# A hybrid RWKV-7 / RG-LRU block: third and fourth lane start their products a step later, and the RG-LRU's last states are transposed elsewhere

## The chip, the core and the metric

One core of one Trainium2 chip runs the whole kernel. A core has a matrix engine (TensorE, PE in the rows), which multiplies out of the on-chip memory SBUF into eight banks of PSUM; VectorE (DVE), ScalarE (ACT) and GpSimd (POOL), which do elementwise work; and SyncE (SP), whose queue issues most of the DMAs between the chip's large memory and SBUF. Each engine has a queue of its own, in the order that the program gives it; an instruction that waits for another engine or for a DMA holds what stands behind it in its queue.

The metric is the device time of one execution in microseconds (us), taken as the median of several runs. Smaller is better.

## What is computed

One step of a diffusion backbone with one layer, on 128 context tokens and 1024 latent tokens (1152 in all, nine tiles of 128), model width 1024. Cut to what matters here:

```python
def block(x, cvec, s0, h0, grid, lp):
    mod = (jax.nn.silu(cvec) @ lp['w_mod'] + lp['b_mod'])[..., None, :]
    sh1, sc1, g1, sh2, sc2, g2 = jnp.split(mod, 6, axis=-1)
    h = rmsnorm(x, lp['ln1_g']) * (1.0 + sc1) + sh1
    proj = h @ lp['w_in']
    r, k, v, xw, xa, xg, xb, gb = jnp.split(proj, SPLITS, axis=-1)
    ya, s_fin = rwkv7_mix(r, k, v, xw, xa, xg, s0, lp['rw_w0'], lp['rw_w_up'], lp['rw_a0'], lp['rw_a_up'],
                          lp['rw_g_up'], lp['rw_k_k'], lp['rw_k_a'], lp['rw_r_k'], lp['rw_lnx_g'], lp['rw_lnx_b'])
    yb, h_fin = rglru_mix(xb, gb, h0, lp['lru_conv_w'], lp['lru_conv_b'], lp['lru_ga_w'], lp['lru_ga_b'],
                          lp['lru_gx_w'], lp['lru_gx_b'], lp['lru_lam'], grid)
    x = x + g1 * (jnp.concatenate([ya, yb], axis=-1) @ lp['w_out'])
    h = rmsnorm(x, lp['ln2_g']) * (1.0 + sc2) + sh2
    u = dwconv(h @ lp['w_up'], lp['ffn_conv_w'], lp['ffn_conv_b'], CONV_F_LEFT, grid)
    ua, ub = jnp.split(u, 2, axis=-1)
    x = x + g2 * ((jax.nn.gelu(ua) * ub) @ lp['w_down'])
    return x, s_fin, h_fin
```

`rwkv7_mix` is a scan over time for 8 heads of 64 in two directions, with one step

```python
def _wkv7_step(S, inp):
    r_t, w_t, kk_t, b_t, k_t, v_t = inp
    sa = jnp.einsum('dbhij,dbhj->dbhi', S, kk_t)
    S = S * w_t[..., None, :] - sa[..., :, None] * b_t[..., None, :] + v_t[..., :, None] * k_t[..., None, :]
    y = jnp.einsum('dbhij,dbhj->dbhi', S, r_t)
    return S, y
```

and `rglru_mix` is a convolution, gates and a linear scan, also in two directions. The block runs on the context from zero states and on the latents from cached states. The outputs are both normalised results, the context's final RWKV states (s_fin) and its final RG-LRU states (h_fin, new_state_lru, 1024 numbers).

## The kernel before

**Stages.** A first stage computes the input projection, and beside it the RG-LRU's scans and gates, the gate g of the RWKV half (products `lg`, copied into `gt`, spilled to `g_d`) and the first part of the RWKV recurrence. The second stage finishes the recurrence, and beside it computes the rest of the modulation (`md`, weights `wmod`), the norm and gate of finished RWKV tiles (`posts`) and the RG-LRU half of the output product (`wout_lru`, products `wo`, weights loaded as `wm` and split into a rounded `woh` and a rest `wol`). Then come the RWKV half of the output product (products `mm`, the mixed rows loaded as `yb`) with the second norm, and the feed-forward part.

**Lanes.** The eight heads are four pairs. A chain takes one pair through chunks of 128 tokens, in 64-row halves for two directions. Four lanes run such chains at once: a and b begin beside the projection, c and d with the second stage. For each step a lane loads `KR`, `TTp`, `VS` (`fetch`) and its keys `BK` (`fetch_keys`, which at its second call also copies KR into `kx` on ScalarE), and `prep` makes the step's own matrices: the product `p<-kx,BK` on TensorE, its mask `G` on VectorE, a scaling of BK on GpSimd, and in a second half the transposes of BK and their copy `Kt`. The chain proper then does products `y`, a solve `c<-R,TTp`, its copy back into `VS`, and the state's update `c<-VS,Kt`. The letter behind p, c, y, kx is the lane.

**Order.** Every part is written as a Python generator that gives way at each `yield`. `run_all` steps the generators of the second stage in proportion to the counts written beside them. The calls are recorded in that order, a scheduler then sets each engine's queue, and buffers and PSUM banks go round in the order in which they were asked for. In the second stage the `p` and `c` products of all four lanes share two banks (2 and 4):

```python
    deal(ya=(3,), yb=(5,), yc=(0,), yd=(1,), pa=two, pb=two, pc=two, pd=two, ca=two[::-1], cb=two[::-1], cc=two[::-1],
         cd=two[::-1], md=(6,), wo=(7,), po=two)
    run_all((lane_a, 98 - LA), (lane_b, 98 - LB), (lane_c, 26), (lane_d, 26), (posts(90), 90),
```

**The last states of the RG-LRU.** `lru_fin` (128 x 8) collects the context's last states. At the end of `rest_of_projection`, the last generator of the first stage, TensorE transposes it into a bank of `lg`, VectorE copies the 8 x 128 result to `lru_o`, and the sync engine spills it to the output.

Of the kernel before, what the change touches and what calls it, by code (L numbers as in the profile page):

```python
# [24 lines left out]
LA = 74  # L25
# [5 lines left out]
def beside_all(*gens):  # L31

    st = [[g, float(n), 0] for g, n in gens]
    while st:
        s = min(st, key=lambda e: e[2] / e[1])
        try:
            next(s[0])
            s[2] += 1
            yield
        except StopIteration:  # L40
            st.remove(s)


def run_all(*gens):
    for _ in beside_all(*gens):
        pass
# [12 lines left out]
def tile_hybrid_step(  # L59
# [9 lines left out]
    V, A, G, PE = nc.vector, nc.scalar, nc.gpsimd, nc.tensor  # L69
    load = nc.sync.dma_start  # L70
    spill = nc.sync.dma_start
# [13 lines left out]
    def bank(name):  # L85
        st = psum[name]
        i = st[0][st[1] % len(st[0])]
        st[1] += 1
        return ps_pool.tile([128, 512], F32, name=name, tag=f"b{i}", bufs=1)
# [28 lines left out]
    def half(i):  # L118
        return slice(64 * i, 64 * i + 64)

    def const(name, *shape):
        return cp.tile(list(shape), F32, name=name)
# [45 lines left out]
    def c2(name="c2", dt=F32):  # L168
        return pr.tile([128, 512], dt, name=name, tag="c2", bufs=NC2)
# [31 lines left out]
    ident = const("ident", 128, 128)  # L201
# [205 lines left out]
    for b in range(4):  # L407
        for j0 in (8, 0):
            ps = mod_mm(2 * b + (j0 == 0))
# [415 lines left out]
    lru_fin = const("lru_fin", 128, 8)  # L825
# [116 lines left out]
    class Background:  # L942


        def __init__(self):
            self.q, self.done = [], set()
# [44 lines left out]
    def rest_of_projection():  # L991
        gens = {"x": lru_x, "t": lru_gates, "g": lru_g, "p": p_xg}
        yield from beside([gens[e[0]](*[int(c) for c in e[1:]]) for e in SEQ], 0, RL, 0)
        while bg_l.step():
            yield
        ps = bank("lg")
        PE.transpose(ps[0:8, 0:128], lru_fin, ident)
        lo_ = c2("lru_o")[0:8, 0:128]
        V.tensor_copy(lo_, ps[0:8, 0:128])
        spill(new_lru.rearrange("a b d (q p) -> (a b d q) p", p=128), lo_)  # L1000


    rs = ExitStack()
# [23 lines left out]
    class Lane:  # L1027


        def __init__(self, pool, k, out=None):  # L1030
            self.out = out or pool
            self.pool, self.k, self.py, self.pc, self.pp = pool, k, "y" + k, "c" + k, "p" + k

        def ring(self, name, n, bufs=2):
# [23 lines left out]
    def fetch_keys(L, q, n_):  # L1058

        cs = slice(128 * n_, 128 * n_ + 128)  # L1060
        bk = L.ring("BK", 256).rearrange("p (d t) -> p d t", d=2)
        load(bk, kb_d[q.f, q.p, :, :, 1, cs])
        if n_ == 1:
            for e in range(2):
                A.activation(L.kx[half(e), :, :, e, :], q.KR[half(e)], AF.Copy)
        q.X[n_] = bk, L.kx[:, :, n_]
# [12 lines left out]
    def prep(L, q, n_):  # L1079

        gm = L.ring("G", 512).rearrange("p (d e t) -> p d e t", e=2, d=2)
        km = L.ring("Kt", 256)
        bk, kx = q.X.pop(n_)
        ps = bank(L.pp)
        for d in range(2):
            mm(ps[:, 256 * d:256 * d + 256], bk[:, d], kx[:, d].rearrange("p e t -> p (e t)"))
        V.tensor_tensor(gm, ps.rearrange("p (d e t) -> p d e t", e=2, d=2),
                        mask[:, :, n_].unsqueeze(2).to_broadcast([128, 2, 2, 128]), op=OP.mult)
        x = 2 * q.p + n_
        G.tensor_tensor(bk, bk, pc_f[q.f][:, :, x:x + 1].to_broadcast([128, 2, 128]), op=OP.mult)  # L1090
        yield
        ps = bank(L.pp)
        for d in range(2):
            PE.transpose(ps[:, 128 * d:128 * d + 128], bk[:, d], ident)
        A.activation(km, ps[:, 0:256], AF.Copy)
        q.G[n_] = gm
        q.K[n_] = km.rearrange("p (d t) -> p d t", d=2)
        yield

    def chain(L, pairs):  # L1100
# [8 lines left out]
        qs = {0: fetch(L, *pairs[0])}  # L1109
        fetch_keys(L, qs[0], 0)  # L1110
        fetch_keys(L, qs[0], 1)
        yield from prep(L, qs[0], 0)
        Sc = None
        for hi, (i, n_) in enumerate(hops):
            f, p = pairs[i]
# [7 lines left out]
            q = qs[i]  # L1123
# [11 lines left out]
            if n_ == 0 and (p < 2):  # L1135
                Sc = next_state()
                if p:
                    s_in = L.ring("Si", 128, 1).rearrange("p (d j) -> p d j", d=2)
                    load(s_in, ins["state_rwkv"][0, 0].rearrange("d (f e) i j -> f (e i) d j", e=2)[f])
                    ps = bank(L.pp)  # L1140
# [27 lines left out]
            ps = bank(L.pc)  # L1168
# [9 lines left out]
            if not last:  # L1178
                ps = bank(L.pc)
# [47 lines left out]
    E, LATE = range(1, 5), range(5, NT)  # L1227
    lane_a = chain(Lane(rp, "a"), [(0, p) for p in E] + [(f, 0) for f in range(4)] + [(2, p) for p in range(1, NT)])
    lane_b = chain(Lane(rp, "b"), [(1, p) for p in E] + [(3, p) for p in range(1, NT)])

    PB = 2
# [11 lines left out]
    LB = 52  # L1243
# [10 lines left out]
    pq = pqs.enter_context(tc.tile_pool(name="pq", bufs=1))  # L1254
# [3 lines left out]
    lcd = lcds.enter_context(tc.tile_pool(name="lcd", bufs=1, side="right"))  # L1258
# [3 lines left out]
    def of_output(name):  # L1262
        return pw if name in ("woh", "wol", "yb", "ybh", "ybl") else p3

    lane_c, lane_d = [chain(Lane(lcd, k, pq), [(f, p) for p in LATE]) for f, k in ((0, "c"), (1, "d"))]

    def p2(name, dt=F32, bufs=2):
        return of_output(name).tile([128, 512], dt, name=name, tag=name, bufs=bufs)
# [60 lines left out]
    def posts(n):  # L1329
        for _ in range(n):  # L1330
            bg_p.step()
            yield
# [55 lines left out]
    def mix_load(j, i):  # L1388
        y = p2("yb", bufs=YB)
        load(y.rearrange("p (f t) -> p f t", f=4),  # L1390
             y_d[4 * j:4 * j + 4, :, 128 * i:128 * i + 128].rearrange("f p t -> p f t"))
        return y
# [20 lines left out]
    def wout_lru():  # L1413

        wo = [wout_row(k, G) for k in range(4, 8)]
        yield
        y = mix_load(1, seq_t[0])
        for a, i in enumerate(seq_t):
            x = row4("x", XP)
            if a < 2:  # L1420
                g = gate_row(pw, 16, min(i, 1), "wo")
            load(x, x_rows(i))
            ys = mix_split(y)
            if a + 1 < NT:
                y = mix_load(1, seq_t[a + 1])
            yield
            for n_ in range(2):
                cs = slice(512 * n_, 512 * n_ + 512)
                ps = bank("wo")
                for k in range(4):  # L1430
                    mix_mm(ps, k, ys, wo, cs)
                    if k == 1:
                        yield
                gated(x[:, cs], p2("tm"), ps, g[:, cs])
                yield
            spill(xa_d[i], x)
        gate_last.append(g)
        for k in range(4):
            wo2.append(wout_row(k, G))
            yield  # L1440
# [1 line left out]
    two = (2, 4)  # L1442
    deal(ya=(3,), yb=(5,), yc=(0,), yd=(1,), pa=two, pb=two, pc=two, pd=two, ca=two[::-1], cb=two[::-1], cc=two[::-1],
         cd=two[::-1], md=(6,), wo=(7,), po=two)
    run_all((lane_a, 98 - LA), (lane_b, 98 - LB), (lane_c, 26), (lane_d, 26), (posts(90), 90),
            (seq(mod_rest(16, 24), beside_all((mod_rest(24, 48), 30), (wout_lru(), 48))), FL))
    bg_p.finish()
    p3x.close()
# [68 lines left out]
    for a, i in enumerate(seq_t):  # L1517
# [5 lines left out]
        for n_ in range(2):  # L1523
            ps = bank("mm")
# [184 lines left out]
    for m in range(NF):  # L1709
        q = Box()  # L1710
        q.m, q.ps = m, {}
        for j, c in first if m == 0 else usual:
# [9 lines left out]
            a, b = CH[c]  # L1722
# [10 lines left out]
    if True:  # L1733
# [17 lines left out]
        f = zf.rearrange("p i k t -> p (i k t)")  # L1751
        g2b, lnf, tm = f[:, 0:2 * D].rearrange("p (q c) -> p q c", q=2), f[:, 2 * D:3 * D], f[:, 3 * D:4 * D]
        load(lnf, ins["lnf_g"].unsqueeze(0).to_broadcast([128, D]))
        for q in range(2):
            for n_ in range(2):
                ps = bank("acc")
# [103 lines left out]
```

## Time and profile before

| what | value |
|---|---|
| median of three runs | 1854.52 us |
| the three runs | 1845.20, 1854.52, 1858.80 us |
| the profiled execution | 1849.17 us |
| its span, from the first to the last instruction | 1847.5 us |
| TensorE busy | 1716.4 us (93%) |
| VectorE, ScalarE, GpSimd busy | 69%, 47%, 39% |
| mean granted TensorE clock | 0.954 of full speed |
| DMA moved | 264.92 MB, 143 GB/s on average |

All rows come from the profiled execution. Its times count from the start of its span. The second stage lies from about 737 to about 957 us. A granted clock of 1.00 is the full clock of TensorE, 0.50 half of it; a figure between means that a stretch holds both.

### The profile page before, as it was taken

Reading aid. Unit: us, or ns where it says so; the run is one execution under the profiler, and the core shown is the slowest. Engines: PE = TensorE matmul, PEld = TensorE weight load, DVE = VectorE, ACT = ScalarE, POOL = GpSimd, SP = SyncE. Lnnn points to the kernel's source line nnn. Section 1 sums busy time; section 2 is a strip of 40 time slices with the busy share of each in tenths; the row PEclk is TensorE's granted clock in tenths of the full one; section 3 lists DMA queues with packets and bytes.
Section 4 is the critical chain, followed back from the end, with each engine's and each line's share of the span. In section 5 each row is a group of like instructions: output and inputs, shape, how many; then the busy total and the mean of one; then the engine's idle time right before and its main releaser. Section 6 shows DMA issues by size and latency. Waiting matters only on the chain.

```text
span 1847.5 us, 35759 instructions
## 1 busy us (share of the span) xinstructions
PE 1716.4 (93%) x13341; PEld 1442.9 (78%) x13341; DVE 1272.2 (69%) x2633; ACT 865.5 (47%) x1787; POOL 721.8 (39%) x742
## 2 busy tenths in 40 slices
PE   5998898888999989899988789999999998999996
PEld 4776676678777778456656689999999998888885
DVE  5458967797477664476788877676767667576764
ACT  6466655643666756333335844444444443121211
POOL 1022423322355344131121166666666663434340
PEclk8898979889999999899999899999999999999998
DMA  9254544443443434867775222222222225558571
GB/s 300 63 163 155 174 139 135 147 147 118 145 122 97 131 104 146 257 194 231 232 254 189 82 64 86 78 72 72 74 79 75 77 73 171 184 159 262 173 252 57
DMA packets 268428, 264.92 MB, mean 143 GB/s; under 512 B 21173, under 2 KB 218448, under 8 KB 268256
## 3 DMA queue, kind: packets, MB, share of 16 engines
q1 hardware_dynamic: 252496, 245.97, 42.1%
q10 hardware_dynamic: 15472, 16.54, 2.7%
q8 instruction: 105, 1.72, 0.4%
q14 instruction: 67, 0.55, 0.1%
q0 software_dynamic: 288, 0.14, 0.0%
HBM read 188.00 MB, written 74.58 MB: 142 GB/s over the span
## 4 chain that ended last, share of the span: by engine, by line
PE 66%; DVE 9%; ACT 3%; DMA 3%; issue 3%; POOL 3%; SPq 0%; ACTq 0%; POOLq 0%; DVEq 0%
PE acc L92 14%; PE x L92 7%; PE y L92 7%; PE z L92 7%; PE mm L92 7%; PE v L92 3%; PE wo L92 3%; PE ya L92 2%; PE lg L92 2%; PE md L92 2%; PE pa L92 2%; PE ca L92 1%; DVE X L501 1%; PE yb L92 1%; DVE gt L499 1%
## 5 line engine op out<-in xcount | busy, mean ns | idle before, releaser
L92 PE MATMUL mm<-h_hi,winp 128*128 128x384 f32 x1056 | 304.4, 358 | 4.9 <-DVE vr L808 3.2
L92 PEld LDWEIGHTS mm<-h_hi,winp 128*128 128x128 f32 x1056 | 198.7, 196 | 26.4 <-issue 14.9
L92 PE MATMUL mm<-h_lo,winp 128*128 128x384 f32 x528 | 187.7, 356 | 3.0 <-DVE h_lo L112 3.0
L112 POOL TENSOR_TENSOR wl<-raw,wh 128x512 fp32r<-128x512 f32 x110 | 155.1, 1412 | 69.7 <-ACT wh L106 69.4
L106 ACT ACTIVATE wh<-raw 128x512 fp32r<-128x512 f32 x110 | 69.5, 633 | 148.3 <-PE z L92 81.0
L92 PE MATMUL x<-f_hi,wh 128*128 128x256 f32 (+1 forms) x352 | 105.8, 301 | 8.9 <-ACT q L1652 5.3
L92 PEld LDWEIGHTS mm<-h_lo,winp 128*128 128x128 f32 x528 | 103.7, 197 | 9.6 <-DVE h_lo L112 4.5
L1090 POOL TENSOR_TENSOR BK<-BK,pc 128x256 f32<-128x256 f32 x72 | 47.8, 664 | 150.5 <-PE pa L92 58.8
L92 PE MATMUL x<-f_lo,wh 128*128 128x256 f32 (+1 forms) x352 | 105.5, 300 | 0.2 <-DVE f_lo L112 0.2
L92 PE MATMUL y<-t_hi,wh 128*128 128x320 f32 (+1 forms) x352 | 104.9, 298 | 0.7 <-DVE q L1657 0.7
L92 PE MATMUL x<-f_hi,wl 128*128 128x256 f32 (+1 forms) x352 | 105.3, 299 | 0.0
L92 PE MATMUL y<-t_lo,wh 128*128 128x320 f32 (+1 forms) x352 | 104.7, 297 | 0.0
L92 PE MATMUL y<-t_hi,wl 128*128 128x320 f32 (+1 forms) x352 | 104.6, 297 | 0.0
L112 POOL TENSOR_TENSOR wl<-S,wh 128x512 fp32r<-128x512 f32 x44 | 57.7, 1311 | 105.6 <-ACT wh L106 105.6
L92 PE MATMUL acc<-f_hi 128*128 128x512 f32 x330 | 91.0, 397 | 3.2 <-ACT zf L1760 3.2
L108 POOL TENSOR_SCALAR t_hi<-raw 128x512 fp32r<-128x512 f32 x66 | 52.9, 804 | 81.6 <-PE acc L92 35.4
L1619 DVE SCALAR_TENSOR_TENSOR zf<-C,fcw,zf 128x567 f32<-128x567 f32 x66 | 63.5, 962 | 23.3 <-ACT zf L1617 23.3
L92 PEld LDWEIGHTS acc<-f_hi 128*128 128x128 f32 x330 | 63.1, 192 | 16.9 <-ACT zf L1760 3.7
L92 PEld LDWEIGHTS x<-f_hi,wh 128*128 128x128 f32 x352 | 67.9, 193 | 9.9 <-ACT q L1652 5.8
L112 DVE TENSOR_TENSOR t_hi<-raw,t_hi 128x512 fp32r<-128x512 f32 x66 | 48.1, 735 | 37.0 <-POOL t_hi L108 37.0
L1617 ACT ACTIVATE zf<-C,colB,fcw 128x576 f32<-128x576 f32 x66 | 57.3, 868 | 28.1 <-DVE C L1689 15.7
L600 POOL TENSOR_TENSOR kd<-kd,rk 128x512 f32<-128x512 f32 (+1 forms) x24 | 32.2, 1342 | 97.0 <-ACT kd L598 96.8
(516 smaller groups left out, 5211.1 us busy)
## 6 DMA issues: line engine op xcount, KB each, us to landing
raw<-in_w_down SPq DMA_DIRECT2D x132, 256.0 KB, 3.1
raw<-in_w_up SPq DMA_DIRECT2D x88, 256.0 KB, 3.0
wmod<-in_w_mod SPq DMA_DIRECT2D x68, 256.0 KB, 4.2
act_d<-zf SPq DMA_DIRECT2D x44, 288.0 KB, 2.2
src<-act_d SPq DMA_DIRECT2D x66, 192.0 KB, 3.8
win<-in_w_in SPq DMA_DIRECT2D x44, 256.0 KB, 3.9
KR<-kb_d SPq DMA_DIRECT2D x36, 256.0 KB, 3.2
VS<-v_d SPq DMA_DIRECT2D x36, 256.0 KB, 3.2
```

What stands on the lines that cost most here:

```text
L92: PE.matmul(out, lhsT, rhs, start=start, stop=stop, skip_group_check=True)
L106: A.activation(hi, src, AF.Copy)
L108: eng.tensor_scalar(hi, src, 1.0, 0.0, op0=OP.mult, op1=OP.add)
L112: eng.tensor_tensor(lo, src, hi.bitcast(F32), op=OP.subtract)
L499: V.tensor_tensor(tv, X[:, q + 1:32, q:q + 1].to_broadcast([128, m, q]), X[:, q:q + 1, 0:q].to_broadcast([128, m, q]), op=OP.mult)
L501: V.tensor_tensor(X[:, q + 1:32, 0:q], X[:, q + 1:32, 0:q], tv, op=OP.add)
L600: G.tensor_tensor(self.kd, self.kd, self.k, op=OP.mult)
L1090: G.tensor_tensor(bk, bk, pc_f[q.f][:, :, x:x + 1].to_broadcast([128, 2, 128]), op=OP.mult)
L1617: A.activation(u, src, AF.Identity, scale=fcw[:, 1, m:m + 1], bias=colb("ffn_conv_b", m))
L1619: V.scalar_tensor_tensor(dv[:, :, 1:64], sv[:, :, 0:63], fcw[:, 0, m:m + 1], dv[:, :, 1:64], op0=OP.mult, op1=OP.add)
```

## The change

Two edits. The transpose, copy and spill of `lru_fin` leave the end of the first stage and come, behind a step of their own, between the output weights and the first load of mixed rows in `wout_lru`; they use the `wo` bank and a buffer of `tm`. And a lane can be given a lag: lanes c and d, with a lag of 1, issue their first loads, give way once, and only then record their first `prep`. Their step counts in `run_all` go from 26 to 27.

```diff
--- before.py
+++ after.py
@@ -993,11 +993,6 @@
         yield from beside([gens[e[0]](*[int(c) for c in e[1:]]) for e in SEQ], 0, RL, 0)
         while bg_l.step():
             yield
-        ps = bank("lg")
-        PE.transpose(ps[0:8, 0:128], lru_fin, ident)
-        lo_ = c2("lru_o")[0:8, 0:128]
-        V.tensor_copy(lo_, ps[0:8, 0:128])
-        spill(new_lru.rearrange("a b d (q p) -> (a b d q) p", p=128), lo_)
 
 
     rs = ExitStack()
@@ -1027,8 +1022,10 @@
     class Lane:
 
 
-        def __init__(self, pool, k, out=None):
+        def __init__(self, pool, k, out=None, lag=0):
             self.out = out or pool
+
+            self.lag = lag
             self.pool, self.k, self.py, self.pc, self.pp = pool, k, "y" + k, "c" + k, "p" + k
 
         def ring(self, name, n, bufs=2):
@@ -1109,6 +1106,8 @@
         qs = {0: fetch(L, *pairs[0])}
         fetch_keys(L, qs[0], 0)
         fetch_keys(L, qs[0], 1)
+        for _ in range(L.lag):
+            yield
         yield from prep(L, qs[0], 0)
         Sc = None
         for hi, (i, n_) in enumerate(hops):
@@ -1262,7 +1261,7 @@
     def of_output(name):
         return pw if name in ("woh", "wol", "yb", "ybh", "ybl") else p3
 
-    lane_c, lane_d = [chain(Lane(lcd, k, pq), [(f, p) for p in LATE]) for f, k in ((0, "c"), (1, "d"))]
+    lane_c, lane_d = [chain(Lane(lcd, k, pq, 1), [(f, p) for p in LATE]) for f, k in ((0, "c"), (1, "d"))]
 
     def p2(name, dt=F32, bufs=2):
         return of_output(name).tile([128, 512], dt, name=name, tag=name, bufs=bufs)
@@ -1414,6 +1413,12 @@
 
         wo = [wout_row(k, G) for k in range(4, 8)]
         yield
+        ps = bank("wo")
+        PE.transpose(ps[0:8, 0:128], lru_fin, ident)
+        fin = p2("tm")[0:8, 0:128]
+        V.tensor_copy(fin, ps[0:8, 0:128])
+        spill(new_lru.rearrange("a b d (q p) -> (a b d q) p", p=128), fin)
+        yield
         y = mix_load(1, seq_t[0])
         for a, i in enumerate(seq_t):
             x = row4("x", XP)
@@ -1442,7 +1447,7 @@
     two = (2, 4)
     deal(ya=(3,), yb=(5,), yc=(0,), yd=(1,), pa=two, pb=two, pc=two, pd=two, ca=two[::-1], cb=two[::-1], cc=two[::-1],
          cd=two[::-1], md=(6,), wo=(7,), po=two)
-    run_all((lane_a, 98 - LA), (lane_b, 98 - LB), (lane_c, 26), (lane_d, 26), (posts(90), 90),
+    run_all((lane_a, 98 - LA), (lane_b, 98 - LB), (lane_c, 27), (lane_d, 27), (posts(90), 90),
             (seq(mod_rest(16, 24), beside_all((mod_rest(24, 48), 30), (wout_lru(), 48))), FL))
     bg_p.finish()
     p3x.close()
```

No instruction is added or removed. What the edits do to the queues is seen in the order of the built programs (no time is in it; each row gives line, operation, output<-inputs, size, count).

TensorE before, at the join of the two stages. The `lg` products and the transpose of `lru_fin` are the last rows of the first stage; pc and pd are first products and transposes of lanes c and d:

```order
L92 MATMUL lg<-sgh,guph 128x384
L92 MATMUL lg<-sgl,guph 128x384
L92 MATMUL lg<-sgh,gupl 128x384
L997 MATMUL lg<-ident,lru_fin 8x128
L92 MATMUL pc<-kxc,BK 128x256 x2
L1094 MATMUL pc<-ident,BK 128x128 x2
L92 MATMUL pd<-kxd,BK 128x256 x2
L1094 MATMUL pd<-ident,BK 128x128 x2
L92 MATMUL pa<-kxa,BK 128x256
L92 MATMUL ca<-R,TTp 64x64 x2
L92 MATMUL md<-wmod,silx 32x512 x2
L92 MATMUL ca<-R,TTp 64x64 x2
```

TensorE after, at the end of the `lg` products:

```order
L1091 MATMUL pb<-ident,BK 128x128 x2
L92 MATMUL ca<-R,TTp 64x64 x2
L92 MATMUL lg<-sgh,guph 128x384
L92 MATMUL lg<-sgl,guph 128x384
L92 MATMUL lg<-sgh,gupl 128x384
L92 MATMUL yb<-S1b,KR 128x128 x2
L92 MATMUL yb<-VS,G 64x64 x4
L92 MATMUL ca<-R,TTp 64x64 x2
L1417 MATMUL wo<-ident,lru_fin 8x128
L92 MATMUL ya<-VS,G 64x64
L92 MATMUL pb<-kxb,BK 128x256 x2
```

and, eight rows on, at the join:

```order
L92 MATMUL lg<-sgh,guph 128x384
L92 MATMUL lg<-sgl,guph 128x384
L92 MATMUL lg<-sgh,gupl 128x384
L92 MATMUL ya<-VS,G 64x64
L92 MATMUL pc<-kxc,BK 128x256 x2
L92 MATMUL pd<-kxd,BK 128x256 x2
L92 MATMUL md<-wmod,silx 32x512 x3
L92 MATMUL pa<-kxa,BK 128x256 x2
L92 MATMUL md<-wmod,silx 32x512
L92 MATMUL cb<-R,TTp 64x64 x4
```

Steps of lanes a and b (ca, ya, pb) and the transpose moved ahead of the last `lg` products; pc and pd follow each other, and their transposes stand further back, among md products.

The sync engine's queue before, from the last spills of `g_d` to lane d's first loads. The first two BK are lane c's, the KR, TTp, VS and BK behind them lane d's:

```order
L773 DMA g_d<-gt 128x1152 x2
L940 DMA y_d<-th 128x1152
L773 DMA g_d<-gt 128x1152 x2
L1000 DMA out<-lru_o 8x128
L1272 DMA lnx<-in_rw_lnx_g 128x512
L1272 DMA lnx<-in_rw_lnx_b 128x512
L1062 DMA BK<-kb_d 128x2x128 x2
L1051 DMA KR<-kb_d 128x2x256
L1052 DMA TTp<-tt_d 128x256
L1054 DMA VS<-v_d 128x2x256
L1062 DMA BK<-kb_d 128x2x128 x2
```

The same queue after. The BK ahead of the second pair of `g_d` spills is lane c's first:

```order
L773 DMA g_d<-gt 128x1152 x2
L940 DMA y_d<-th 128x1152
L1059 DMA BK<-kb_d 128x2x128
L773 DMA g_d<-gt 128x1152 x2
L1271 DMA lnx<-in_rw_lnx_g 128x512
L1271 DMA lnx<-in_rw_lnx_b 128x512
L1059 DMA BK<-kb_d 128x2x128
L1048 DMA KR<-kb_d 128x2x256
L1049 DMA TTp<-tt_d 128x256
L1051 DMA VS<-v_d 128x2x256
L1059 DMA BK<-kb_d 128x2x128 x2
```

One load of keys moved ahead of two spills, and the spill of `lru_o` went away.

The sync engine's queue before, at the last output weights (`wm`) of the second stage and the first mixed rows (`yb`) of the next:

```order
L1381 DMA wm<-in_w_out 128x512
L1324 DMA y_d<-gd 128x2x128
L1381 DMA wm<-in_w_out 128x512 x2
L1436 DMA xa_d<-x 128x1024
L1286 DMA gd<-g_d 128x2x128
L1381 DMA wm<-in_w_out 128x512 x2
L1324 DMA y_d<-gd 128x2x128
L1390 DMA yb<-y_d 128x4x128
L1511 DMA x<-xa_d 128x1024
```

and after:

```order
L1389 DMA yb<-y_d 128x4x128 x2
L1441 DMA xa_d<-x 128x1024
L1340 DMA wmod<-in_w_mod 128x512 x2
L1285 DMA gd<-g_d 128x2x128
L1284 DMA v<-v_d 128x2x128
L1323 DMA y_d<-gd 128x2x128
L1516 DMA x<-xa_d 128x1024
L1380 DMA wm<-in_w_out 128x512
L1285 DMA gd<-g_d 128x2x128
L1380 DMA wm<-in_w_out 128x512
L1441 DMA xa_d<-x 128x1024
L1380 DMA wm<-in_w_out 128x512 x3
```

The first two yb stand ahead of the last five wm, and the last spill xa_d is followed by three wm where it was followed by two.

## Rows read from the trace of the kernel before

**Rows 1.** The profile's page, part 1: busy time, share of the span, instructions.

```profile
PE 1716.4 (93%) x13341; PEld 1442.9 (78%) x13341; DVE 1272.2 (69%) x2633; ACT 865.5 (47%) x1787; POOL 721.8 (39%) x742
```

**Rows 2.** Windows: length, TensorE busy (instructions), granted clock, DMA share, GB/s.

```profile
736.00:744.00 8.00, 1.24 (x6) 0.71 0.91 296
744.00:755.00 11.00, 9.49 (x32) 0.59 0.74 239
755.00:776.00 21.00, 21.00 (x147) 1.00 0.75 237
776.00:806.00 30.00, 25.55 (x250) 0.94 0.57 184
806.00:957.00 151.00, 150.70 (x1250) 1.00 0.74 237
957.00:985.00 28.00, 16.73 (x69) 0.76 0.77 246
```

**Rows 3.** Timeline of TensorE: start, duration, line, output<-inputs, shapes, count [idle before, releaser].

```profile
733.86 0.45 PE L92 MATMUL lg<-sgh,guph 128*128 128x384 f32 x1 [1.64 <-ACT gt L771]
...
736.61 0.27 PE L997 MATMUL lg<-ident,lru_fin 128*8 128x128 f32 x1
743.63 2.05 PE L92 MATMUL pc<-kxc,BK 128*128 128x256 f32 x4 [6.76 <-DMA BK<-kb_d]
746.44 0.69 PE L1094 MATMUL pc<-ident,BK 128*128 128x128 f32 x2 [0.75 <-DVE G L1087]
...
749.58 0.69 PE L1094 MATMUL pd<-ident,BK 128*128 128x128 f32 x2 [0.75 <-DMA wmod<-in_w_mod]
...
751.05 0.48 PE L92 MATMUL ca<-R,TTp 64*64 64x64 f32 x4
...
755.31 1.13 PE L92 MATMUL pb<-kxb,BK 128*128 128x256 f32 x4
...
768.27 1.13 PE L92 MATMUL pc<-kxc,BK 128*128 128x256 f32 x4
```

**Rows 4.** Timeline of the sync engine's queue, 732 to 743 us.

```profile
732.44 0.32 SPq L940 DMA_DIRECT2D y_d<-th  x1
...
737.57 0.30 SPq L1000 DMA_DIRECT2D out<-lru_o  x1
...
738.97 1.19 SPq L1062 DMA_DIRECT2D BK<-kb_d  x2
740.20 0.61 SPq L1051 DMA_DIRECT2D KR<-kb_d  x1
...
741.98 1.18 SPq L1062 DMA_DIRECT2D BK<-kb_d  x2
```

**Rows 5.** DMA issues, 725 to 750 us: count, KB each, median us to landing.

```profile
BK<-kb_d SPq DMA_DIRECT2D x5, 128.0 KB, 4.5
```

**Rows 6.** Timeline of ScalarE, 732 to 754 us.

```profile
732.27 0.56 ACT L1075 ACTIVATE R<-yb 64x128 f32<-64x128 f32 x2 [1.17 <-PE yb L92]
...
744.75 1.28 ACT L1065 ACTIVATE kxd<-KR 64x512 f32<-64x512 f32 x2 [3.62 <-DMA KR<-kb_d]
...
753.56 0.57 ACT L1075 ACTIVATE VS<-ca 64x128 f32<-64x128 f32 x2 [2.87 <-PE ca L92]
```

**Rows 7.** Timeline of GpSimd, around the first rounding of output weights.

```profile
792.82 0.62 POOL L1090 TENSOR_TENSOR BK<-BK,pc 128x256 f32<-128x256 f32 x1 [4.68 <-PE pb L92]
793.40 2.22 POOL L108 TENSOR_SCALAR woh<-wm 128x512 fp32r<-128x512 f32 x3
```

**Rows 8.** Timeline of TensorE, first products of the next stage.

```profile
967.61 0.76 PE L92 MATMUL mm<-woh,ybh 128*128 128x512 f32 x1 [4.83 <-ACT rv L128]
...
970.05 0.79 PE L92 MATMUL mm<-woh,ybl 128*128 128x512 f32 x1 [1.25 <-DVE ybl L112]
```

**Rows 9.** Timeline of the sync engine's queue, last output weights.

```profile
956.57 0.91 SPq L1381 DMA_DIRECT2D wm<-in_w_out  x2
958.63 0.33 SPq L1436 DMA_DIRECT2D xa_d<-x  x1
```

## The prediction

> **What bounds the kernel now.** I read the page's engine table first: TensorE is busy for 93% of the span and no other engine for more than 69% [rows 1]. So time can only be won where TensorE waits or runs at the lower clock, and only if nothing later takes the gain back. The windows show where that is [rows 2]. From 806 to 957 us, most of the stage of the four lanes, TensorE is busy for 150.70 of 151 us at full clock, and from 755 to 776 all the time. Three stretches that the diff touches are not dense: the join of the projection and this stage (736 to 755 us: busy 1.24 of 8 and 9.49 of 11 us, clocks 0.71 and 0.59), the start of the RG-LRU's output product (776 to 806 us: 25.55 of 30) and the hand-over to the next stage (957 to 985 us: 16.73 of 28).
>
> TensorE's timeline names the waits of the join [rows 3]. Work ends with the transpose of lru_fin at 736.88. The next instruction, lane c's first product, starts at 743.63 after 6.76 us of idling that ended when its keys BK had landed. Lane c's transposes wait 0.75 us for G, then lane d's product and transposes follow with another 0.75, and only behind them come steps of lanes a and b (ca, pb), although lane b's R had been copied at 732.27 [rows 6]. They stand there since the four lanes share two banks, in program order. Behind the idle time the clock is lower: pc's four instructions take 2.05 us, against 1.13 at 768.27.
>
> The sync engine's queue says why BK was late [rows 4]. It is issued at 738.97, behind the spills of g, the spill of lru_o and two loads of norm rows; pc starts 4.66 us later, and the transfers of this stretch list 4.5 us to landing for BK's 128 KB [rows 5], with the DMA engines 91% busy from 736 to 744 [rows 2].
>
> **The change part by part.** *RG-LRU's last states.* The same transpose (0.27 us), the same small copy and the same 4 KB spill are issued elsewhere. On the sync engine the spill leaves the place ahead of lane c's and d's loads: 0.30 us of issue, 0.47 to the start of the next row [rows 4]. On TensorE the transpose falls into the wait of 1.64 us before 733.86 [rows 3]. In its new place the spill stands on the sync engine between loads of the output weights and waits there for its copy on VectorE; wmod loads, output-weight loads, yb and a load of keys are queued behind it. GpSimd begins to round the first of these weights at 793.40 only [rows 7], and the transpose that feeds the copy stands among the lg products, so I cost the wait at nothing. Without that cover it costs the lateness of one copy of 8 rows, below 1 us.
>
> *Lanes c and d a step later.* In the changed order lane a's ca and ya and lane b's pb stand among the last lg products, pc and pd directly behind each other, and their transposes some fifteen rows later among md products. On the sync engine's queue lane c's first keys stand ahead of the last two spills of g. The sum by steps:
>
> 1. End of lg. Lane a's ca (0.48 for half of it, so 0.96 at most), pb (1.13) and the transpose (0.27) come among the lg products: 2.36 us, of which 0.27 stood at their end before and 1.64 fills the wait for gt [rows 3]. So lg ends some 0.5 us later, at about 737.4. ScalarE's copies of VS (0.57, rows 6 show them at 753.56) come ahead of the last gt and can put these off by as much.
> 2. pc. BK is issued behind y_d, at 732.44 + 0.32 = 732.8, and lands 4.66 later, at 737.4. So pc follows lg with hardly a gap, at full clock (1.13), and ends at 738.5.
> 3. pd. It stands next and nothing passes it. It needs lane d's KR, the copy kxd, and its keys. KR was issued at 740.20, the copy began 4.55 later, when it had landed, and took 1.28 [rows 4, 6]. Ahead of KR the queue loses the lru_o spill (0.47) and one BK (half of 1.19) and gets up to 0.57 from step 1: issue at about 739.7, copy done at 745.5. Lane d's keys go out 1.78 us behind KR as before, at 741.5, and land at 746.0 by 4.5. I take 745.7. So the gap isn't closed. It moves from pc to pd and is as long (738.5 to 745.7, 7.2 us against 6.76), and I expect the lower clock behind it again.
> 4. Sum. Work starts again 745.7 − 743.63 = 2.1 us later, but less stands behind the gap: pc (2.05), two waits for transposes (0.75 each, now beside md products), ca (0.96) and pb (1.13), 5.6 us. The join gives **−3.5 us**. Its ends: 0, if lane d's last operand lands 3.5 us later than I take, as the last of a full DMA; and −9, if it arrives with lane c's (6.76 + 1.5 + 0.9 of clock on pc).
>
> Behind 755 TensorE is dense, so what is saved there stays saved unless a new wait appears.
>
> *The start of the output product.* The first rounding at 793.40 stands on GpSimd behind a BK of lane b that waited 4.68 us for pb [rows 7]; the changed order has this BK behind the first rounding. TensorE idles for 30 − 25.55 = 4.45 us in the stretch [rows 2], the most that can come back, and a new order can add as much. I take −0.5.
>
> *The hand-over.* The first product of the next stage waits 4.83 us, the first that reads ybl 1.25 [rows 8]. In the changed order the first two yb are issued ahead of the last five weight loads, which could win up to 6.1; against that the last spill xa_d stands ahead of three weight loads, where it was two. I take −0.5, between −6.1 and +4 (rival C).
>
> In all −4.5 us. The profiled execution took 1849.17 us, 1.67 more than its span and 5.35 less than the median of 1854.52 (runs from 1845.20 to 1858.80). That makes 1844.7 for such an execution and **1850** for the median.
>
> A rule bears on the gap. After 6.76 us without work the granted clock was 0.59, after the wait of 1.64 us no instruction shows a lower one [rows 2, 3]. The Trainium skill, page "TensorE: Matmul & The Clock Gate", section "Why this matters for your kernels", says to keep matmuls back to back, as waits for a DMA between them bring the clock down; the trace agrees. By it nothing of the clock is won here, since the gap stays as long, while a clock that stayed up would make the sum about 2 us better (0.9 for each of two lanes' products).
>
> **The rivals.** *(A) The gap moves and nothing is won.* For it: the DMA engines are 91% busy from 736 to 744, so lane d's last operand may come with the same last byte whatever the order, and products put ahead can delay gt and with it the g spills ahead of KR. Against: ca and pb have their data early and run in a gap that exists. That the new order only renames who waits belongs here. Result 0: 1854.5.
>
> *(B) The later waits go too.* An earlier first rounding lets output products fill 776 to 806, and early yb closes the hand-over's waits: −3.5 − 0.7 × 4.45 − 0.7 × 6.1, about −11: 1843.5. For it GpSimd's rows. Against: TensorE had work for 25.55 of these 30 us, so a lane's chain through other engines and not the weights may set the waits.
>
> *(C) Slower, by the hand-over.* The last weights come through three buffers. With xa_d ahead of three loads, the sixth waits for the last tile's sum: from about 957.0 (the second of the pair at 956.57) to behind xa_d, 958.63 + 0.33 [rows 9], 2 us, and the two behind it lose 2 us more to their round trips, while the join gives nothing: +4, 1858.5. It decides from the point where the last weights, and no longer yb, are what the first products of the next stage wait for.
>
> **How the numbers follow.** My forecast has 0.50, (A) 0.22, (B) 0.13, (C) 0.15. The likeliest gives 1850; its steps are uncertain by about 3 us, and a median of three runs by some 4, as the spread of the runs shows. The range that holds 8 in 10 reaches from a little beyond (B) to a little beyond (C): 1841 to 1860. One per cent of 1854.5, about what a measurement of this kernel can tell from no change, is 18.5 us. No case gets there: the waits of the three stretches, with 2 us of clock, are 6.8 + 1.5 + 1.6 + 2 + 4.5 + 6.1, some 22 us, and nearly all would have to go. Faster by over 1% gets 0.05, slower 0.03, for waits that no row of before shows and for uneven runs; 0.92 is within.
>
> **What would show it.** Right: pc starts before 738.5 and takes 1.1 us; a gap of 6 to 8 us stands before pd and is ended by kxd or BK; a clock near 0.6 follows it; pb's product of 755.31 stands before 737; the dense stretch that ended near 957 ends 3 to 4 us sooner. Wrong: if pd starts before 743, the gain is twice mine; if lg ends after 739 or pd starts after 748, there is none; if the first rounding of output weights stays near 793, (B) is out; if the first product of the next stage waits for wol or woh, (C) is in.

## The result and the profile after

The changed kernel takes 1863.12 us in the median of 12 runs (1855.86 to 1867.12), the kernel before 1852.98 us (1845.2 to 1858.8). The ratio is 1.0051, with a 95% interval of 1.0034 to 1.0067: 10 us slower, outside the range that I gave and against its sign. The profiled execution took 1860.33 us, its span is 1858.6.

The page's engine line after, and TensorE's windows (length, busy and instructions, clock, DMA share, GB/s) for the join, the dense stretch behind it, the start of the output product, the rest of the stage, and the hand-over:

```profile
PE 1719.8 (93%) x13341; PEld 1442.7 (78%) x13341; DVE 1273.7 (69%) x2633; ACT 864.1 (46%) x1787; POOL 719.2 (39%) x742
```

```profile
741.00:758.00 17.00, 8.72 (x33) 0.70 0.85 286
758.00:784.00 26.00, 26.00 (x168) 1.00 0.89 277
784.00:810.00 26.00, 20.05 (x148) 0.80 0.31 100
810.00:958.00 148.00, 147.98 (x1249) 1.00 0.75 238
958.00:1001.00 43.00, 27.86 (x163) 0.84 0.63 202
```

Read against [rows 2], with one shift: the last product of the projection, in a part with the same instructions in both kernels, starts at 729.8 here and at 723.6 before. So 6.2 us of the two profiles' distance of 11.1 arise before the change begins. The stretch of 806 to 957 us was dense before and is dense now. The stretch of small products behind the join is worse than before: 5.95 us idle in 26 at a clock of 0.80, where it was 4.45 in 30 at 0.94.

TensorE's timeline at the join and at the hand-over, the counterpart of [rows 3, 8] (6.2 us are to be taken off for the join):

```profile
738.59 0.27 PE L1417 MATMUL wo<-ident,lru_fin 128*8 128x128 f32 x1
...
743.66 1.13 PE L92 MATMUL pc<-kxc,BK 128*128 128x256 f32 x4
...
752.66 2.05 PE L92 MATMUL pd<-kxd,BK 128*128 128x256 f32 x4 [7.87 <-DMA BK<-kb_d]
...
969.61 0.48 PE L92 MATMUL mm<-woh,ybh 128*128 128x512 f32 x1
...
981.22 0.80 PE L92 MATMUL mm<-woh,ybl 128*128 128x512 f32 x1 [10.47 <-DVE ybl L112]
```

Pc no longer waits, pd does; and the first products of the next stage start at once, but the third of them waits 10.47 us for ybl, in the place of 4.83 and 1.25 before. (Mixed rows yb are split like the weights, into a rounded ybh and a rest ybl, which VectorE makes.) The sync engine's queue and ScalarE at the join ([rows 4, 6]):

```profile
738.95 0.52 SPq L1059 DMA_DIRECT2D BK<-kb_d  x1
...
741.98 2.37 SPq L773 DMA_DIRECT2D g_d<-gt  x2
...
746.41 0.61 SPq L1048 DMA_DIRECT2D KR<-kb_d  x1
...
748.19 1.18 SPq L1059 DMA_DIRECT2D BK<-kb_d  x2
```

```profile
750.93 1.28 ACT L1062 ACTIVATE kxd<-KR 64x512 f32<-64x512 f32 x2 [1.12 <-DMA KR<-kb_d]
```

The last states in their new place, their copy on VectorE and the spill in the sync engine's queue:

```profile
780.89 0.27 DVE L1419 COPY tm<-wo 8x128 f32<-8x128 f32 x1
```

```profile
782.34 0.47 SPq L1285 DMA_DIRECT2D gd<-g_d  x1
782.90 0.30 SPq L1420 DMA_DIRECT2D out<-tm  x1
```

The copy was done at 781.16, 1.7 us before the queue came to the spill, so the spill held nothing up.

GpSimd at the start of the output product ([rows 7]), and VectorE's last weight and ybl at the hand-over:

```profile
785.27 0.62 POOL L108 TENSOR_SCALAR woh<-wm 128x512 fp32r<-128x512 f32 x1
800.04 0.63 POOL L1087 TENSOR_TENSOR BK<-BK,pc 128x256 f32<-128x256 f32 x1 [14.15 <-PE pb L92]
800.64 1.20 POOL L108 TENSOR_SCALAR woh<-wm 128x512 fp32r<-128x512 f32 x2
```

```profile
978.54 0.68 DVE L112 TENSOR_TENSOR wol<-wm,woh 128x512 fp32r<-128x512 f32 x1
...
980.49 0.68 DVE L112 TENSOR_TENSOR ybl<-yb,ybh 128x512 fp32r<-128x512 f32 x1
```

One weight half is rounded 14 us earlier than before (by the shift), and the next stands behind a BK that waits 14.15 us for pb, so nothing is won by it. At the hand-over ybl stands in VectorE's queue behind the last rest of the weights, wol.

### The profile page after: what moved, and what is told of

It is laid out like the page before. It is cut to its first block, busy times and chain, and to the rows that moved or that the text cites. A ratio compares the mean times of both kernels' runs of the same rounds, so it can differ in the third digit from the quotient of the medians.

```text
span 1858.6 us, 35758 instructions
## 1 busy us (share of the span) xinstructions
PE 1719.8 (93%) x13341; PEld 1442.7 (78%) x13341; DVE 1273.7 (69%) x2633; ACT 864.1 (46%) x1787; POOL 719.2 (39%) x742
## 4 chain that ended last, share of the span: by engine, by line
PE 67%; DVE 8%; ACT 4%; POOL 2%; DMA 2%; issue 2%; SPq 0%; ACTq 0%; POOLq 0%; DVEq 0%
PE acc L92 14%; PE mm L92 7%; PE x L92 7%; PE y L92 7%; PE z L92 7%; PE v L92 3%; PE wo L92 3%; PE md L92 2%; PE lg L92 2%; PE ya L92 2%; PE pa L92 2%; PE yb L92 2%; PE ca L92 1%; PE pb L92 1%; DVE gt L499 1%
```

## The experiments

All ratios are to the kernel before, measured beside each on the same chip, with their 95% intervals. "Idle" is TensorE's idle time from one microsecond before the end of the last output product wo to the 48th product mm of the next stage, and "runs" is into how many unbroken runs the 64 md products of the stage fall in TensorE's queue. The kernels e1, e3, e6, e7, e9, e11, e13, e15 and the change have the lag.

| kernel | ratio | idle at the hand-over, us | runs |
|---|---|---|---|
| the change | 1.0051 [1.0034, 1.0067] | 15.1 | 33 |
| the change, again (e12) | 1.0057 [1.0037, 1.0077] | 16.4 | 33 |
| lag alone (e1) | 1.0016 [0.9999, 1.0032] | 11.8 | 31 |
| last states moved, with their step, alone (e2) | 1.0034 [1.0015, 1.0052] | 15.7 | 34 |
| both, without the added step (e3) | 1.0033 [1.0017, 1.0049] | 11.1 | 33 |
| before with a bare step (e5) | 1.0056 [1.0036, 1.0076] | 14.4 | 37 |
| change, first yb ahead of the spill (e6) | 1.0042 [1.0025, 1.0060] | 14.8 | 32 |
| change, spill on ScalarE's queue (e7) | 1.0020 [1.0006, 1.0034] | 16.0 | 32 |
| before, first loads of c and d from ScalarE (e8) | 1.0024 [1.0005, 1.0043] | 11.8 | 34 |
| change, share 52 (e9) | 1.0015 [0.9995, 1.0036] | 10.4 | 33 |
| before, weights in pairs (e10) | 1.0007 [0.9988, 1.0026] | 13.4 | 28 |
| change, weights in pairs (e11) | 1.0023 [1.0002, 1.0044] | 15.0 | 27 |
| change, share 52 and pairs (e13) | 0.9987 [0.9973, 1.0001] | 10.9 | 28 |
| bare step, share 52 (e14) | 1.0017 [0.9999, 1.0035] | 13.4 | 34 |
| lag alone, pairs (e15) | 0.9996 [0.9978, 1.0015] | 9.7 | 27 |
| before | 1 | 11.3, and 12.1 (e4) | 33 |

**Taking the change apart.** My theory after the first result (T) was that the new step and spill cost at the hand-over and that the lag wins; the rival (R) that the lag makes lanes c and d late. *Lag alone* keeps the lag and puts the five lines of the last states back.

> Only lanes c and d lag; the last states of the RG-LRU are transposed and spilled at the end of the projection as before. Theory T (what costs is the new step of wout_lru and the spill in the midst of the weight loads, which put the output product's weights and the last products back, while the lag wins 3 to 5 us at the join): ratio 0.996 to 0.999. Rival R (the lag makes lanes c and d late and the stage ends late for that): ratio 1.003 to 1.007, like the change. Rival N (the two edits only reshuffle the order and either alone may cost): within 0.999 to 1.003 for one of them.

1.0016: neither the gain of T nor the loss of R; it is what I had written for the third case. *The move alone* keeps the five lines and their step in wout_lru, with lag 0 and 26 steps.

> Only the transpose, copy and spill of the last states move, with their step; no lag. Theory T: 1.003 to 1.006, the wait for the first keys at the join stays near 6.3 us (0.5 less, for the spill's place on the sync engine), and the weights' rounding or the hand-over to the next stage is later than before. Rival R: 0.999 to 1.001.

1.0034, with the wait for the keys at 6.63 us and 15.7 us idle at the hand-over: as T says. The two parts, 1.0016 and 1.0034, add up to the change's ratio. But in this kernel the spill does wait for its copy, which it doesn't in the change (sync engine's queue, line waited for, total, times, longest):

```profile
SPq L1420 <- DVE tm L1419: 9.9, 1, 9.9
```

*Both without the step* takes the `yield` behind the spill away.

```diff
         spill(new_lru.rearrange("a b d (q p) -> (a b d q) p", p=128), fin)
-        yield
         y = mix_load(1, seq_t[0])
```

> The whole change, but the transpose, copy and spill share a step with the first load of mixed rows, so wout_lru has as many steps as before. Theory T in its narrower form (the extra step ends wout_lru a step late): 0.996 to 0.999. If the place of the spill itself costs: 1.002 to 1.005. Rival R: 1.003 to 1.007.

The idle time at the hand-over is back at 11.1, but the ratio is 1.0033, so the narrower form of T missed: without the step a loss remains. It is not a wait of the spill, whose copy was done at 778.18, ahead of its turn in the queue at 779.97. From the projection's last product to the 48th product mm of the next stage TensorE idles for 26.1 us here, 26.0 and 27.1 in the two profiles of before, and is busy for 245.1 against 237.9 and 241.8: what is lost is busy time, and this run doesn't say by which order.

**Chance.** The kernel before, profiled again:

> The kernel before, profiled once more. If the 6 us by which the changed kernel's profile is behind already at 730 us, in a part with the same instructions, are chance, this profile differs from the first one by some us there as well; if they belong to the change, it agrees with the first within 1.5 us at 730.

Its span is 1858.6 us, 11.1 more than that of the profile which the prediction read, and the last product of the projection starts at 729.6, against 723.6. So the shift of 6 us that stood against the change belongs to chance. TensorE's windows in this second profile, at the join, the stretch behind, and the hand-over:

```profile
741.00:758.00 17.00, 8.70 (x27) 0.53 0.84 277
...
783.00:813.00 30.00, 25.76 (x217) 0.84 0.53 167
...
957.00:999.00 42.00, 29.90 (x185) 0.88 0.75 235
```

In the second window, the start of the output product, the idle time agrees (4.24 of 30 us here, 4.45 in [rows 2]) but the clock doesn't: 0.84 against 0.94 in a stretch with the same instructions. One profile tells the waits of this kernel to within a microsecond or so and its time only to within ten. From here on I compare waits between profiles, and times by the medians.

**The step.** *A bare step* puts nothing but one `yield` between the weights and the first yb into the kernel before.

> The kernel before with nothing but one more step in wout_lru, between the output weights and the first load of mixed rows; the last states stay where they were. Theory S (the step is what costs: it puts the first yb behind weight loads that wait for free buffers, so the first output product comes 4 to 10 us later and the stage ends later): 1.002 to 1.005, first output product 68 us or more behind the end of the lg products, where it was 62 to 66. Rival P (the spill itself or its wait on the sync engine costs): 0.999 to 1.001.

1.0056, as much as the whole change and a little above what I had written for S: the step costs, with nothing in it. The idle time at the hand-over is 14.4 us, and the md products fall into 37 runs instead of 33; TensorE spends 38.4 us on them (from the start of each to the start of the next instruction, without idling), against 33.2 and 34.2 in the two profiles of before. The long wait of the hand-over is there too, here before `po`, the transposes of `posts`, which read osq from VectorE (engine line waited for, total, times, longest):

```profile
PE po L1321 <- DVE osq L1317: 10.3, 1, 10.3
```

*The first yb ahead of the spill* and *the spill on ScalarE's queue* (`spill_a` for `spill`) are two narrower versions.

> The whole change, with the first load of mixed rows ahead of the transpose and spill instead of behind their step. Theory S: the first output product is back at 60 to 66 us, and the ratio falls from 1.005 to about 1.002, that of the lag alone. If the place of the first yb does not matter: 1.004 to 1.006.

> The whole change, with the spill issued on ScalarE's queue, so that the sync engine doesn't wait for the copy. Rival P: 1.001 to 1.003. Theory S: 1.004 to 1.006, since yb stays behind the weight loads.

With yb first, the first output product is back at 61.3 us behind the end of lg (69.7 in the change), but the ratio stays at 1.0042: where the output product begins isn't what counts, and that part of my theory S fell. With the spill on ScalarE 1.0020, better than the change, as rival P had it. But P's reason isn't there: in the change the spill waits for nothing (its copy was done 1.7 us before its turn, and 2.0 us in the second profile). This kernel's sync queue also lets a load of wmod pass ahead of weights; whether that is the gain isn't shown, and the idle time at the hand-over stays at 16.0.

*The share.* A step more leaves wout_lru's declared 48 steps as they are, so it is stepped as before and ends behind the lanes. I raised the share in the changed kernel, and then in the one with the bare step:

```diff
-            (seq(mod_rest(16, 24), beside_all((mod_rest(24, 48), 30), (wout_lru(), 48))), FL))
+            (seq(mod_rest(16, 24), beside_all((mod_rest(24, 48), 30), (wout_lru(), 52))), FL))
```

> The whole change, with wout_lru's share of steps counted as 52 instead of 48, so that it ends sooner against the lanes; the last y products of three lanes then stand behind the last output product again, as before the change. Theory H (the added step ends the output product behind the lanes, so nothing is left to run while the last weights come): idle time at the hand-over 11 to 13 us instead of 15, ratio 1.001 to 1.003. Rival (the hand-over is not what costs): 15 us of idling or a ratio of 1.004 to 1.006.

> The kernel before with the bare step of the earlier experiment and wout_lru's share at 52; the y products stand behind the last output product again, and the md products in 34 runs instead of 37. Theory H: idle time at the hand-over 10 to 12 us instead of 14.4, ratio 1.000 to 1.003 instead of 1.0056. If the step costs by its place and not by the end of wout_lru: 1.004 to 1.007.

1.0015 and 1.0017, from 1.0051 and 1.0056. In the change the idle time falls to 10.4 us, from 15.1 and 16.4, with as many runs as before it: theory H. With the bare step it falls by 1.0 us only, to 13.4, and misses what I had named for H, while the runs fall from 37 to 34 and the time on md products from 38.4 to 36.2 us. So there the share helps too, but not shown to be by the hand-over. TensorE behind the last output product of e9, which ends at 966.0:

```profile
966.17 1.06 PE L92 MATMUL md<-wmod,silx 128*32 128x512 f32 x6
967.16 0.45 PE L92 MATMUL ya<-VS,G 128*64 128x64 f32 x8
967.44 0.40 PE L92 MATMUL yc<-VS,G 128*64 128x64 f32 x8
967.67 0.40 PE L92 MATMUL yd<-VS,G 128*64 128x64 f32 x8
968.00 1.06 PE L92 MATMUL md<-wmod,silx 128*32 128x512 f32 x6
...
980.09 0.79 PE L92 MATMUL mm<-woh,ybl 128*128 128x512 f32 x1 [4.99 <-DVE ybl L112]
```

Seven md products (14 records, two for each) and the y products of three lanes stand there, in the change four md products and no y.

**The gap at the join.** Lanes c and d of the kernel before load their first operands from ScalarE's queue (`fetch` and `fetch_keys` take the queue as an argument).

> The kernel before with the first loads of lanes c and d (KR, TTp, VS, both BK) issued on ScalarE's queue, so that they don't stand behind the spills of g. If the order of the sync engine's queue makes the gap at the join: the gap of 6.8 us falls below 3 us and the ratio is 0.994 to 0.998. If full DMA engines make it: the gap stays over 5 us and the ratio is 0.999 to 1.002. It can also cost, 1.001 to 1.003, by 10 issues of about 0.5 us ahead of the last gt on ScalarE.

The one gap of 6.76 us becomes two, with the lg products that are still to come in between:

```profile
743.09 1.19 PE L92 MATMUL pc<-kxc,BK 128*128 128x256 f32 x2 [3.97 <-DMA BK<-kb_d]
...
754.18 1.10 PE L92 MATMUL pd<-kxd,BK 128*128 128x256 f32 x4 [2.67 <-DMA BK<-kb_d]
```

Their sum is as long, and lg ends 19.4 us behind the start of the projection's last product instead of 13.0 and 14.0: issues on ScalarE stand among the copies gt. The kernel is slower, 1.0024, as the third case had it. A gap here can be moved, but neither version closed it.

**Broken runs.** The rows of the changed kernel show that one md product takes as long as four in a row (two records are one product):

```profile
773.90 1.04 PE L92 MATMUL md<-wmod,silx 128*32 128x512 f32 x2
...
958.88 1.07 PE L92 MATMUL md<-wmod,silx 128*32 128x512 f32 x8
```

Four products go to four strips of 32 rows of one bank. A bare step has 37 runs where the kernel before has 33. So I loaded the rows of w_mod two by two, which makes the scheduler keep more of them together:

```diff
-                raw.append(p2("wmod", bufs=6))
-                load(raw[k], ins["w_mod"][0, 128 * k:128 * k + 128, 128 * idx:128 * idx + 512])
+                if k % 2 == 0:
+                    wide = of_output("wmod").tile([128, 2, 512], F32, name="wmod", tag="wmod", bufs=3)
+                    load(wide, ins["w_mod"][0, 128 * k:128 * k + 256, 128 * idx:128 * idx + 512].rearrange("(a p) c -> p a c", p=128))
+                raw.append(wide[:, k % 2])
```

> The kernel before with the modulation's weights loaded in pairs of rows, one DMA for two. In TensorE's queue the 64 md products of this stage then stand in 28 unbroken runs instead of 33. If a run of one to four of them takes about 1 us however many it holds, as the rows of before and after show: 4 to 6 us less, ratio 0.996 to 0.998. If what counts is the number of products: 0.999 to 1.002.

> The changed kernel with the same pairs: 27 runs instead of 33. If runs count: 5 to 7 us less than the changed kernel, ratio 1.001 to 1.003 to the kernel before; else 1.004 to 1.006.

On the kernel before nothing, 1.0007, against what I expected: the time that TensorE spends on md products does fall from 33.2 and 34.2 us in the two profiles of before to 28.7, but 13.4 us of idling at the hand-over take some 1.7 of it back, and the rest isn't seen in the median. On the changed kernel that time falls from 36.9 and 35.8 to 30.0 us, and the median is 7.6 us lower than in e12, measured beside it, 1855.38 against 1862.99, as written for the case that runs count. Last, the versions that join the threads:

> The whole change with wout_lru's share at 52 and the modulation's weights loaded in pairs (28 runs of md products instead of 33). If the hand-over and the broken runs are what the change loses: 0.996 to 0.999, below both kernels. If the lag itself costs some us by a way not found yet: 1.000 to 1.003.

> The lag alone, with the last states where they were, and the modulation's weights in pairs (27 runs). If the lag's gain at the join is kept where no step is added and runs are whole: 0.995 to 0.998. If the stretch at 786 to 806 us takes it back: 0.999 to 1.002, with 5 us idle and over 4 us of clock lost there.

0.9987 is the lowest ratio of all, in the range for the first case; its interval just reaches 1, so a version that beats the kernel before isn't shown, and one that beats the changed kernel is. The lag with whole runs gives 0.9996, the second case, with 5.0 us idle and 4.7 of clock lost in its stretch. The repeat of the change:

> The changed kernel once more, timed and profiled a second time. Its ratio should be 1.003 to 1.007 again; its profile tells chance from what belongs to the kernel: the wait for lane d's keys at the join and the long wait at the hand-over should come again within 1 us, the clock's loss around 785 to 810 us may differ by some us, as in the two profiles of before.

1.0057. The wait for lane d's keys is 7.9 us again, the wait for ybl 11.05, and the clock of the stretch behind the join is lower still (windows of the second profile, the stretch of 784 to 810 above):

```profile
778.00:804.00 26.00, 20.68 (x139) 0.68 0.27 86
```

## Why the prediction was wrong

**Right: the four steps of the join.** Taken off the 6.2 us of shift, lg ended at 737.3 (I had 737.4), pc started at 737.5 and took 1.13, pd at 746.5 (745.7) behind a gap of 7.87 (7.2). The clock behind it was low, pd took 2.05. What TensorE loses there, idle plus busy time times the missing clock, summed over windows of 2.5 us and the 30 us from 8 us before the last lg, is 10.0 + 3.9 and 10.2 + 6.1 us in the two profiles of before, 8.9 + 2.2 and 8.6 + 1.5 in the two of after: 4.5 us less on average, where I had said 3.5. Over all profiles it is 12.4 us on average in the ten with the lag and 15.9 in the six without (e8 left out, as its loads go another way): 3.6 less. Rival (A), that the gap moves and nothing is won, is half right: it moves, and something is won. Right as well was the wait of the spill at nothing; but "below 1 us" for a late copy was not: in e2 the copy ended at 795.57, and the spill had waited 9.9 us.

**Wrong: "so what is saved there stays saved unless a new wait appears", and the −0.5 for the start of the output product.** The 40 us from 45 to 85 us of the same count lose 4.8 + 1.4 and 4.8 + 4.9 us before and 6.0 + 4.9 and 5.3 + 7.7 after: 4 us more on average, most of it clock. The two profiles of before differ by 3.5 us in this stretch's clock, but over the same ten and six profiles it is 10.6 against 7.7: 2.9 more with the lag. So the gain at the join is about given back here, and no run with the lag is shown to be faster than before: lag alone is 1.0016, 0.9996 with whole runs of md. The sign that I had named, a dense stretch that ends 3 to 4 us sooner, didn't come: from the projection's last product to the end of the last output product it is 232.1 and 237.1 us before, 237.1 and 237.9 after.

**Wrong: the −0.5 for the hand-over.** It measured +4 of idle time (15.1 and 16.4 against 11.3 and 12.1). I had two things in the sum, yb that is issued earlier and xa_d ahead of the last weights, and took them from the sync engine's queue. What counts is a chain that I hadn't followed. From the end of the last output product to the end of the last wol it takes 11.5 us in both profiles of before, 12.3 and 12.9 in those of after, 12.7 in e9: buffers of woh come free with the last output products, and loads, roundings and rests follow one another. Ybl stands behind wol on VectorE, so the earlier yb was no gain. The chain is 11.1 to 13.4 us long in all profiles but one (e13, 15.2). The windows from the end of the last output product to the first product that reads ybl, and from there to the 48th product, before:

```profile
955.76:970.05 14.29, 6.22 (x52) 0.69 0.86 279
970.05:987.55 17.50, 14.29 (x51) 0.86 0.64 199
```

after, and in its second profile (e12):

```profile
966.90:981.22 14.32, 3.85 (x29) 0.70 0.76 267
981.22:1000.38 19.16, 14.49 (x51) 0.87 0.53 154
```

```profile
961.64:976.54 14.90, 3.85 (x28) 0.72 0.79 261
976.54:999.09 22.55, 17.21 (x51) 0.73 0.44 129
```

So the first window is about as long before and after (14.4 in the second profile of before, 14.1 in e9), and what changes is how much TensorE work is left to fill it: 6.2 and 5.8 us before, 3.9 after, 7.3 in e9. The y products of three lanes, 0.9 us, stand behind the last output product before (955.76 is its end) and ahead of it after:

```profile
955.69 0.45 PE L92 MATMUL ya<-VS,G 128*64 128x64 f32 x8
...
956.20 0.40 PE L92 MATMUL yd<-VS,G 128*64 128x64 f32 x8
956.54 1.06 PE L92 MATMUL md<-wmod,silx 128*32 128x512 f32 x8
```

```profile
964.97 0.34 PE L92 MATMUL yd<-VS,G 128*64 128x64 f32 x4
...
966.52 0.39 PE L92 MATMUL wo<-woh,ybl 128*128 128x512 f32 x1
```

The rest of the difference between before and after is the same instructions at the lower clock (the first mm took 0.76 us before, 0.48 after), so not all of the +4 is lost time. The second window is 1.7 to 5.1 us longer after (17.4 in the second profile of before), with idle time of 4.7 and 5.3 us against 3.2 and 3.5, and in e12 with a clock of 0.73. In e9 it is 17.7. The result is on rival (C)'s side; it priced +4 at the right place. Its mechanism, weights held behind xa_d, can be at most the 0.8 to 1.4 us by which the chain is longer, and e9, with two of these loads behind xa_d as before, has 12.7 too.

**Not costed: the step.** The change says that the last states come "behind a step of their own", and I priced the transpose, the copy and the spill, but not the `yield`. It makes wout_lru one step longer with its share unchanged. A bare step costs as much as the whole change, and in the change a share of 52 takes most of it back, together with 5 to 6 us of idle time at the hand-over. That the step costs by the end of wout_lru is shown for this much, in the change. It isn't shown for the bare step, whose idle time the share lowers by 1.0 us only and which has the 37 runs, some 4 to 5 us more on md products. And e3, without the step, doesn't come back to the lag's 1.0016.

**What stays open.** From the projection's last product to the 48th product of the next stage the two profiles of before take 263.9 and 268.9 us, those of after 270.6 and 275.3: 6.6 on average, against 10 between the medians. Of these 6.6, 3.6 are idle time (26.0 and 27.1 before, 30.0 and 30.3 after) and the rest is busy time, which differs by 4 us between two profiles of one kernel. Outside, the instructions are the same, and profiles of the same part differ by up to 12 us, so that I can't say where the other 3 are. Nor is it known which order makes e3 busy for longer, or what makes e7 better than the change.

## What to carry to other kernels

Where generators are interleaved by declared shares, a `yield` is an edit with a price: look in the built order at which generator now ends last, and at what is left to run beside the serial chain that starts with its end. Closing a gap is worth what the later stretches let stand, so sum idle time and lost clock over the whole stage, not at the gap. And profile the unchanged kernel twice before believing a term of a few microseconds.

## What was not expected of the hardware

One md product of 32 output rows takes 1.04 us and four in a row, into different strips, 1.07; another product between them breaks that. The 64 products of the stage took 28.7 us in 28 runs (e10), 33.2 and 34.2 in 33 (before), 38.4 in 37 (e5). And the clock fell without a long wait: in the changed kernel it was 0.50 from 791.9 to 796.9 us, where TensorE was busy for 4.34 of 5 us, and from 781.9 on no single wait was longer than 0.7 us. The windows of these 10 us:

```profile
786.90:791.90 5.00, 3.78 (x43) 0.98 0.00 0
791.90:796.90 5.00, 4.34 (x27) 0.50 0.00 0
```
